# Two mixers that project the unnormed x: the norm's factor moves from the operands to the drains

## The chip, the cores and the metric

The kernel runs on one core of one Trainium2 chip. The metric is the device time of one execution of the program in microseconds (us), as the median of several runs. The engines are named as in the profile: PE (TensorE matmul) with PEld (its weight load), DVE (VectorE), ACT (ScalarE), POOL (GpSimd) and SP (SyncE), which here only issues DMAs.

## What is computed

A decoder trunk of two layers over 1024 tokens of width 1024, in float32. Cut to what matters:

```python
def rmsnorm(x, g):
    return x * rsqrt(mean(x * x, axis=-1) + EPS) * g

for l in range(2):
    if l == 1:
        shared = nsa_shared_kv(x, g_kv, w_kv, ...)         # norm of x, keys and values, compressed blocks
    mem_k, mem_v = split(rmsnorm(mem, g_mem[l]) @ w_mem_kv[l])   # 256 memory tokens, 4 heads of 128
    h = rmsnorm(x, g_mix[l])
    if l == 0:                                              # "mix A"
        q, k, v, r, alr, mq = split_cols(h @ a_w_in, [256, 256, 512, 512, 16, 512])
        log_a = log_sigmoid(alr @ w_alpha + b_alpha) / 16
        o = rmsnorm(gla_chunked(q, k, v, log_a), g_head) * silu(r)
    else:                                                   # "mix B"
        q, gates, mq = split_cols(h @ b_w_in, [512, 24, 512])
        o = nsa_attend(q, sigmoid(gates), *shared)
    x = x + concat([o, mem_attend(mq, mem_k, mem_v)]) @ w_out
    x = x + conv_ffn(rmsnorm(x, g_ffn[l]), ...)             # 1024 -> 2 x 2816 -> 1024
return rmsnorm(x, g_final)
```

The norm multiplies each token by one number, rs = 1 / sqrt(mean of squares + EPS). A projection is linear in its input, so (rs x g) @ W and rs (x g @ W) are the same but for rounding.

## The kernel before

**Tiles.** x stands with the 1024 channels as eight tiles of 128 partitions and the 1024 tokens as columns; all work goes in two halves of 512 tokens (`HT`), one after the other. A float32 product is made of three fast ones: each operand is split into a rounded part (`...r`, made on ACT) and the rest (`...l`, made on DVE: source minus rounded part), and PE multiplies r by r, r by l and l by r. So a weight tile of 128 x 1024 (`wtile`, `wload`) costs one ACT and one DVE pass (lines 176 and 177), a tile of h one ACT and one DVE pass of 512 columns (`rl`, lines 224, 225, or 227, 228 where a gain is multiplied in), and one projection of 128 output channels for one half (`projg`, lines 192 to 194) is 24 matmuls of 512 columns into one of eight PSUM banks. What takes the bank's result to SBUF is called its drain.

**The norm.** `Norm.add` squares a tile on ACT (line 256) and adds it up in two accumulators (`nacc`, line 266), one on DVE and the other on POOL where `pool` is true. `done` puts the sum over channels through PE (`ms`, line 278), and `inv_rms` (lines 239 to 244) makes rs as a tile of 128 equal rows, so a factor for each column. `gained` then makes hf = x rs for each of eight tiles, the odd ones on POOL, the others on DVE (line 285), and h is the split of hf.

**The stages, in order.** At the program's start `mix_a` projects the memory: `MemKV.project` multiplies the unnormed, split memory `mh` with four key weight tiles (`mk`: 96 matmuls of 256 columns) and then with four value weight tiles (`mv`: 48 of 512 columns), and takes the memory's norm in where it drains (`mkf`, line 363, and `mV`). Woven into it are the statistics (`stats`) and the normed h (`first_norm`) of x's first half. Then `qkv_a` projects keys and queries (`qk`, drained into `gk` and `gq`), the low rank gate input (`alr` into `aT`) and the values (`gv` into `vt`). For each half `gla` runs the gated linear attention: gate product z, cumulated sums b (lines 681 to 700), then seven levels, in each of which DVE makes an operand (`dec`, lines 709 to 715, and `z`, line 721), PE multiplies (`lev`, line 741) and DVE copies under a mask into `A` (line 748). Beside it `fill` yields other work of PE: the gates r (`gate_gen`: `gr` into `sr`), the memory queries (`mem_query`: `mq`), h and `qkv_a` of the second half. The output projection, the ConvFFN of layer 0 (`ffn`) and its `after_ffn0` follow. The last products of the ConvFFN are `dn` (`d` is the generator that yields them), drained by adding them to x (line 1348); beside them `after_ffn0` takes statistics, hf and h of both halves and the memory projection `MemKV(1)`. `mix_b` begins with `kc`, the keys and values that are to be compressed, and the branch gates, then memory queries, the selection's keys, values, queries `q2` and the attention. Output projection, ConvFFN of layer 1 and final norm close the program.

**What sets the order.** A scheduler puts each engine's instructions in a fixed row. It takes them from the generators in the order in which `weave` and `take` run them: `weave((a, 40.0), (b, 101.0))` draws from both so that they progress in step over their stated lengths. An engine works off its row strictly in order. Loads are issued by SP (weights, and x in `stats` by POOL), and the transfers of one issuer's queue follow each other. Buffers come from pools: 14 of 512 columns (`U`), 32 of 1024 (`V`), six for split weights (`wrl`), four for raw weights (`raw`).

Of the kernel before, what the change touches and what calls it, by code (L numbers as in the profile page):

```python
# [10 lines left out]
AF = mybir.ActivationFunctionType  # L11
# [23 lines left out]
def kernel(  # L35
# [88 lines left out]
    nc.gpsimd.dma_start(cs, cst)  # L124
# [111 lines left out]
    def inv_rms(ms, n):  # L236
        y = U(s="rs")
        a = U(s="rt")
# [8 lines left out]
    class Norm:  # L247
# [23 lines left out]
        def done(self):  # L271
            ms = PS("ms")[:, : self.w]
            if len(self.acc) == 2:
                nc.vector.tensor_tensor(self.acc[1], self.acc[1], self.acc[0], ALU.add)
                self.acc = self.acc[1:]
            n = len(self.acc)
            for j in range(n):
                mm(ms, on_d, self.acc[j], start=(j == 0), stop=(j == n - 1))
            return inv_rms(ms, self.w)

# [112 lines left out]
    class MemHead:  # L393
# [3 lines left out]
        def query(self, w, h):  # L397
            pq = PS("mq")
            yield from projg(pq, w, h)
            self.q = rl(pq, scale=-(P**-0.5), s="mq")  # L400
# [82 lines left out]
    def mem_query(mkv, jobs, att, gain=None):  # L483
        for hd, wsrc, hh in jobs:
            w = wtile(wsrc, "wmq", gain)
            for half, h in hh:
                m = MemHead(mkv, hd, half)
                yield from m.query(w, h)
# [100 lines left out]
    def mix_a():  # L589
        mkv = MemKV(0)  # L590
        mkv.load(nc.sync)
# [4 lines left out]
        def stats(half, xt):  # L596
            n = Norm(pool=half == 1)
            tvs = []
            for k2 in range(4):
                t = V(s="x0")  # L600
                tv = t.rearrange("p (k t) -> p k t", k=2)
                last_x[0] = nc.gpsimd.dma_start(tv, x[2 * k2 : 2 * k2 + 2, :, hs(half)].rearrange("k p t -> p k t"))
                tvs.append(tv)
            for tv in tvs:
                for i in range(2):
                    n.add(tv[:, i, :])
                    if half == 0:
                        xt.append(tv[:, i, :])
                    yield 1.0
            xt.append(n.done())  # L610
            yield 1.0

        def first_norm(half, h, xt):
            get = (lambda k: xt[k]) if half == 0 else reload(x, 1, nc.gpsimd)
            yield from gained(get, xt[-1], C_MIX, h)

        def qkv_a(h, after=None):
            kt, qt = V(s="gk"), V(s="gq")
            for q, t in enumerate((kt, qt)):
                for hp in range(2):  # L620
                    w = wtile(a_w[2 * (1 - q) + hp], "wqk")
                    ps = PS("qk")
                    yield from projg(ps, w, h)
                    src = ps.rearrange("p (c t) -> p c t", c=4)
                    dst = t.rearrange("p (c h t) -> p c h t", c=4, h=2)[:, :, hp, :]
                    nc.scalar.activation(dst, src, AF.Copy, scale=(1.0, 0.125)[q])
# [4 lines left out]
            nc.scalar.activation(aT[0:64, :], pa[0:64, :], AF.Copy)  # L631
# [23 lines left out]
        def gate_gen(h, sr):  # L655
            srv = [V(s="sr") for _ in range(2)]
            for r in range(4):
# [4 lines left out]
                nc.scalar.activation(s, ps, AF.Copy)  # L662
# [194 lines left out]
        xt = [[], []]  # L857

        def start():
            yield from stats(0, xt[0])  # L860
            yield from first_norm(0, h[0], xt[0])
# [5 lines left out]
        follow(nc.gpsimd.dma_start(idu, kst[:, : 2 * P]), last_raw[0], "order")  # L867
# [4 lines left out]
        weave((qkv_a(h[0], last_x[0]), 45.0), (stats(1, xt[1]), 12.0))  # L872
        om0 = []
        op0 = out_proj(a_wo, 0, x, nn[0], om0)
        for half in range(2):
            sr = []

            def fill():
                jobs = [(hd, a_w[8 + hd], [(half, h[half])]) for hd in range(4)]
                yield from gate_gen(h[half], sr)  # L880
                att = Attend(4)
                if half == 0:
                    both = blend(
                        (mem_query(mkv, jobs, att), 21.0), (later(15.0, first_norm(1, h[1], xt[1])), 15.0 + 10.0)
                    )
                    yield from beside(both, att, 4, 3)
                    yield from beside(qkv_a(h[1]), att, 0, 3)
                else:
                    yield from beside(mem_query(mkv, jobs, att), att, 4, 3)
# [4 lines left out]
            weave((gla(half, *self_out[half], sr), (40.0, 36.0)[half]), (fill(), (101.0, 84.0)[half]))  # L894
# [4 lines left out]
    def ffn(l, blocks_, after):  # L899
# [3 lines left out]
        nn = [Norm(w) for _, w in ends]  # L903
# [459 lines left out]
    def after_ffn0(d, nn, segs=None):  # L1363
        hh = [[], []]

        def prep(half):
            rs = nn[half].done()
            yield 1.0
            yield from gained(lambda k: xs[k][:, hs(half)], rs, None, hh[half], (1, 3, 5, 7))

        drain(take(d, 5))
        drain(take(d, 7))
        p0 = prep(0)
        mkv = MemKV(1)
        weave((take(d, 3), 8.1), (take(p0, 2), 2.0))
        mkv.load(nc.sync)
        mkv.square(nc.gpsimd)
        weave((d, 27.0), (take(p0, 5), 20.0))

        def both():  # L1380
            yield from p0
            yield 2.0
            yield from prep(1)

        weave((both(), 20.0), (mkv.project(), 36.0))
        for k in range(KT):
            xs[k] = None
        return mkv, hh

    def mix_b(mkv, h):  # L1390
# [15 lines left out]
        def comp_in(kind, half, ps):  # L1406
            pv = ps.rearrange("p (m j) -> p j m", j=16)
# [18 lines left out]
        for half in range(2):  # L1426
            for kind in range(2):
                ps = PS("kc")
                proj(ps, wkc[kind], h[half])
# [4 lines left out]
            nc.scalar.activation(t[0:64, :], pg[0:64, :], AF.Copy)  # L1434
            gsb.append(t)

# [20 lines left out]
        def keys(kind):  # L1457
            def evac(half, ps):
# [34 lines left out]
        def mem_all():  # L1493
            yield from beside(mem_query(mkv, mem_jobs, att, G_B), att, 5, 2)
# [3 lines left out]
        weave((mem_all(), 76.0), (compress(), 15.0))  # L1498
# [32 lines left out]
        def queries(m):  # L1531
            def evac(half, ps):
# [17 lines left out]
        def values(half, cs_):  # L1550
# [14 lines left out]
            for ps, c in zip(pv, cs_):  # L1565
                if val[half] is None:
                    val[half] = V(s="val")
                nc.scalar.activation(val[half][:, c * 256 : (c + 1) * 256], ps[:, :256], AF.Copy)
# [321 lines left out]
```

## Time and profile before

| | |
|---|---|
| median of 3 runs | 2359.45 us (2358.92 to 2360.3) |
| profiled execution | 2364.08 us |
| its span in the trace | 2362.0 us |
| PE busy | 2272.0 us, 96% |
| DVE busy | 1728.7 us, 73% |
| ACT busy | 1129.2 us, 48% |
| POOL busy | 506.7 us, 21% |

The profile comes from one execution, so times in it are compared with each other and with its own 2364.08 us. "Busy" is the time in which an engine has an instruction; a PE that is busy may still run at half its clock, which the granted clock shows (1.00 is the full one, and a mean below 1.00 in a stretch is a mix of the two levels, 2.4 and 1.2 GHz). A row of the timeline that ends in brackets names how long the engine had been idle before it and what released it. In names such as `mk<-mh,wmkr` the result stands left and the operands right.

### The profile page before, as it was taken

To read this page: it belongs to the slowest core of one execution; us is meant where nothing else is said; L and a number is where in the kernel's file an instruction comes from. 1 tells how busy PE (TensorE), PEld (TensorE's weight loads), DVE (VectorE), ACT (ScalarE), POOL (GpSimd) and SP (SyncE) were. 2 spreads that over 40 slices of the span, in tenths; PEclk is the share of its full clock that TensorE was granted. 3 is DMA by queue.
4 is the path that set the end of the run, shared out by engine and by line. 5 is a ranking of instruction groups with operands and counts; after the bars stand their busy time and mean duration, and the time that the engine had idled before them with its cause. 6 is when DMAs were issued, how large, how long until landed. Compare 5 with 4: busy or idle time off the path is not lost.

```text
span 2362.0 us, 31229 instructions
## 1 busy us (share of the span) xinstructions
PE 2272.0 (96%) x11030; PEld 1845.7 (78%) x11030; DVE 1728.7 (73%) x2988; ACT 1129.2 (48%) x2066; POOL 506.7 (21%) x429
## 2 busy tenths in 40 slices
PE   6989999999999999999899999999989999999997
PEld 5877877777788888887788877767777788888875
DVE  7496585978777768878555588874968777768786
ACT  6445544543343335455444588774543343335443
POOL 3222211313422210013202121110313422210011
PEclk9999999999999999999999999999999999999998
DMA  6213236433433229544231111017433433229432
GB/s 239 94 50 117 64 111 206 140 111 134 138 103 107 96 90 337 178 134 148 65 92 58 44 34 45 8 57 227 135 107 134 138 103 107 101 87 341 155 97 94
DMA packets 138221, 284.95 MB, mean 121 GB/s; under 512 B 16022, under 2 KB 22211, under 8 KB 138064
## 3 DMA queue, kind: packets, MB, share of 16 engines
q1 hardware_dynamic: 128992, 260.11, 33.5%
q0 software_dynamic: 4464, 14.46, 1.8%
q10 hardware_dynamic: 4608, 8.39, 1.0%
q8 instruction: 86, 1.41, 0.2%
q14 instruction: 71, 0.58, 0.1%
HBM read 211.06 MB, written 71.83 MB: 120 GB/s over the span
## 4 chain that ended last, share of the span: by engine, by line
PE 77%; DVE 11%; DMA 4%; issue 3%; ACT 3%; POOL 1%; SPq 1%; DVEq 0%; POOLq 0%; ACTq 0%
PE dn L1301 5%; PE dn L1302 5%; PE dn L1300 5%; PE fy L974 4%; PE fy L976 4%; PE fy L975 4%; PE no L1694 3%; PE fw L976 3%; PE fw L974 3%; PE fw L975 3%; PE fx L974 2%; PE fx L975 2%; PE fx L976 2%; PE npt L1678 2%; DMA wu<-in_w_up_dram 2%
## 5 line engine op out<-in xcount | busy, mean ns | idle before, releaser
L1300 PE MATMUL dn<-db,da 128*128 128x512 f32 (+1 forms) x628 | 243.0, 389 | 4.0 <-ACT db L1229 2.1
L1301 PE MATMUL dn<-db,da 128*128 128x512 f32 (+1 forms) x628 | 243.5, 388 | 2.6 <-DVE db L1230 2.6
L1302 PE MATMUL dn<-db,da 128*128 128x512 f32 (+1 forms) x628 | 243.3, 388 | 0.0
L974 PE MATMUL fy<-B,Ah 128*128 128x512 f32 x496 | 196.6, 396 | 14.9 <-DVE q L1008 7.5
L976 PE MATMUL fy<-B,Al 128*128 128x512 f32 x496 | 195.8, 395 | 2.5 <-DVE Al L939 2.5
L975 PE MATMUL fy<-B,Ah 128*128 128x512 f32 x496 | 195.1, 393 | 0.0
L938 ACT ACTIVATE Ah<-wu 128x1024 fp32r<-128x1024 f32 x124 | 130.3, 1052 | 108.5 <-PE fy L975 62.5
L958 POOL TENSOR_TENSOR wu<-wu,wu 128x512 f32<-128x512 f32 x44 | 61.3, 1394 | 558.6 <-DVE Al L939 305.0
L266 POOL TENSOR_TENSOR nacc<-nacc,nsq 128x512 f32<-128x512 f32 (+1 forms) x30 | 49.0, 1634 | 596.9 <-ACT nsq L256 596.7
L939 DVE TENSOR_TENSOR Al<-wu,Ah 128x1024 fp32r<-128x1024 f32 x124 | 160.7, 1297 | 20.7 <-ACT Ah L938 20.4
L1300 PEld LDWEIGHTS dn<-db,da 128*128 128x128 f32 x628 | 118.9, 189 | 29.1 <-issue 2.7
L1301 PEld LDWEIGHTS dn<-db,da 128*128 128x128 f32 x628 | 118.9, 189 | 27.6 <-DVE db L1230 3.3
L976 PE MATMUL fw<-B,Al 128*128 128x512 f32 x352 | 137.7, 391 | 0.0
L1302 PEld LDWEIGHTS dn<-db,da 128*128 128x128 f32 x628 | 118.7, 189 | 23.8 <-issue 0.2
L975 PE MATMUL fw<-B,Ah 128*128 128x512 f32 x352 | 137.1, 389 | 0.0
L974 PE MATMUL fw<-B,Ah 128*128 128x512 f32 x352 | 137.0, 389 | 0.0
L1230 DVE TENSOR_TENSOR db<-bl,db 128x512 fp32r<-128x512 f32 x154 | 107.9, 701 | 30.2 <-ACT db L1229 29.6
L974 PEld LDWEIGHTS fy<-B,Ah 128*128 128x128 f32 x496 | 94.1, 190 | 40.3 <-DVE q L1008 11.7
L976 PEld LDWEIGHTS fy<-B,Al 128*128 128x128 f32 x496 | 94.4, 190 | 24.5 <-DVE Al L939 4.4
L1229 ACT ACTIVATE db<-bl 128x512 fp32r<-128x512 f32 x154 | 95.7, 621 | 31.8 <-PE dn L1302 24.5
L975 PEld LDWEIGHTS fy<-B,Ah 128*128 128x128 f32 x496 | 94.1, 190 | 19.2
L192 PE MATMUL op<-om,wor 128*128 128x512 f32 x256 | 102.1, 400 | 0.9 <-ACT om L224 0.9
(416 smaller groups left out, 6289.5 us busy)
## 6 DMA issues: line engine op xcount, KB each, us to landing
wu<-in_w_up_dram SPq DMA_DIRECT2D x176, 256.0 KB, 2.9
bl<-gb_d SPq DMA_DIRECT2D x154, 256.0 KB, 2.8
gb_d<-fc SPq DMA_DIRECT2D x132, 256.0 KB, 3.0
wb<-in_w_down_dram SPq DMA_DIRECT2D x44, 256.0 KB, 4.2
wa<-in_w_down_dram SPq DMA_DIRECT2D x22, 512.0 KB, 7.8
xre<-om_d SPq DMA_DIRECT2D x32, 256.0 KB, 4.4
wo<-in_a_wo_dram SPq DMA_DIRECT2D x16, 512.0 KB, 3.6
x_r<-x SPq DMA_DIRECT2D x32, 256.0 KB, 2.5
```

The source lines that it names most:

```text
L192: mm(ps, wr[:, k, :], hr, start=(k == 0), stop=False)
L938: a = nc.scalar.activation(hi, src, AF.Copy)
L939: b = nc.vector.tensor_tensor(lo, src, f(hi), ALU.subtract)
L974: mm(ps, wr, hr, start=(first and j == 0), stop=False, skip_group_check=True)
L975: mm(ps, wr, hl, start=False, stop=False, skip_group_check=True)
L976: mm(ps, wl, hr, start=False, stop=(stop and j == 3), skip_group_check=True)
L1229: nc.scalar.activation(w[:, hs(0)], t, AF.Copy)
L1230: b = tt(w[:, hs(1)], t, f(w)[:, hs(0)], ALU.subtract)
L1300: mm(o, hi, bh, start=first, stop=False, skip_group_check=True)
L1301: mm(o, hi, bl, start=False, stop=False, skip_group_check=True)
L1302: mm(o, lo, bh, start=False, stop=stop or n == NP - 1, skip_group_check=True)
L1694: mm(acc[a * 64 : a * 64 + 64, :256], v, pf[:, a * 256 : (a + 1) * 256], start=(n == 0), stop=(n == last[a]),)
```

## The change

The norm's factor leaves the operands. h is now the split of x itself (in mix A of x times its gain column, which rides along in `rl`), and rs is multiplied in where PSUM is drained, as a product of the bank with the factor's tile on DVE. Values, whose drain has the tokens on the partitions, need the factor by token: `Norm.by_token` makes it with 16 small matmuls (`mst`, one column each) into `rst`, and ACT's drain takes it as its scale. With that hf and its products go, for 32 tiles of h.

The order moves too. At the start x's first half is loaded by SP, tile by tile, with the first weight tile `w0` behind the first; the first projection follows at once, and the statistics come behind h. The memory of layer 0 is loaded later, and its projection is the first thing that `fill` yields in the first GLA half. At the end of the ConvFFN of layer 0 h of the first half is taken while the `dn` products run; `kc` follows them directly, with h and the norm of the second half woven in; the memory projection of layer 1 comes later, in `mem_all`. In `ffn` and `stats` the norms' additions are all on DVE (`pool=False`), and the additions of the memory's norm of layer 1 move from POOL to DVE. The table of constants `cs` is loaded by ACT's queue instead of POOL's.

```diff
     def mix_a():
...
-        def stats(half, xt):
-            n = Norm(pool=half == 1)
+        def stats(half, h=None):
+            n = Norm(pool=False)
...
-                last_x[0] = nc.gpsimd.dma_start(tv, x[2 * k2 : 2 * k2 + 2, :, hs(half)].rearrange("k p t -> p k t"))
+                if half == 0:
+                    for i in range(2):
+                        last_x[0] = nc.sync.dma_start(tv[:, i, :], x[2 * k2 + i, :, hs(half)])
+                        if k2 + i == 0:
+                            w0.append(wraw(a_w[2], s="wqk"))
...
+                    if h is not None:
+                        h.append(rl(tv[:, i, :], col(C_MIX + 2 * k2 + i), s="h"))
...
+            rs[half] = n.done()
+            rst[half] = n.by_token()
...
+            def evac(ps, q, hp):
+                t = (kt, qt)[q]
+                src, sc = (a.rearrange("p (c t) -> p c t", c=4) for a in (ps, rs[half]))
+                dst = t.rearrange("p (c h t) -> p c h t", c=4, h=2)[:, :, hp, :]
+                nc.vector.scalar_tensor_tensor(dst, src, (1.0, 0.125)[q], sc, ALU.mult, ALU.mult)
...
-                    nc.scalar.activation(v[:, hs(i)], pv[2 * c2 + i], AF.Copy)
+                    c = 2 * c2 + i
+                    nc.scalar.activation(v[:, hs(i)], pv[c], AF.Copy, scale=rst[half][:, c : c + 1])
...
-                nc.scalar.activation(s, ps, AF.Copy)
+                nc.vector.tensor_tensor(s, ps, rs[half], ALU.mult)
...
-        pj, st = mkv.project(), start()
-        for g, n in ((pj, 1), (st, 4), (pj, 1), (st, 8 - 4), (pj, 1), (st, 1), (pj, 1)):
-            drain(take(g, n))
-        weave((pj, 16.0), (st, 16.0))
...
+        st = stats(0, h[0])
+        drain(take(st, 16))
...
+        qa = qkv_a(0, h[0], last_x[0])
+        drain(take(qa, 8))
+        drain(st)
+        mkv.load(nc.sync)
+        weave((qa, 38.0), (stats(1), 12.0))
...
-                yield from gate_gen(h[half], sr)
+                if half == 0:
+                    yield from mkv.project()
+                yield from gate_gen(half, h[half], sr)
...
-            weave((gla(half, *self_out[half], sr), (40.0, 36.0)[half]), (fill(), (101.0, 84.0)[half]))
+            weave((gla(half, *self_out[half], sr), (40.0, 36.0)[half]), (fill(), (132.0, 84.0)[half]))
...
-        nn = [Norm(w) for _, w in ends]
+        nn = [Norm(w, False) for _, w in ends]
...
     def after_ffn0(d, nn, segs=None):
...
+        drain(take(d, 9))
+        weave((take(d, 6), 16.2), (take_x(0, range(4)), 4.0))
+        weave((take(d, 4), 10.8), (take_x(0, range(4, 8)), 4.0))
+        drain(norm(0))
+        drain(d)
...
+        weave((front(0), 14.0), (second, 9.0))
+        mkv = MemKV(1)
+        mkv.load(nc.sync)
+        drain(front(1))
+        mkv.square(nc.vector)
...
-        weave((mem_all(), 76.0), (compress(), 15.0))
+        weave((mem_all(), 107.0), (compress(), 15.0))
```

The drains that are left out above read alike: `query` (16 tiles `mqs`), `comp_in` (4 `kcs`), the branch gates (2 `gsb`), `keys` (4 `ksf`) and `queries` (8 `qf`) each multiply the bank by `rs[half]` on DVE before what they did before, and `aT` (2) is such a product now.

Three places show the new order. First ACT at the program's start, before and then with the change; `wmkr` and `wqkr` are rounded parts of weight tiles, `mh` the split memory, `nacc` and `nsq` squares of x.

```order
L176 ACTIVATE wmkr_124<-wmk_93 128x1024
L227 ACTIVATE mh_103<-mem_95,cs 128x256 x2
L227 ACTIVATE mh_108<-mem_96,cs 128x256 x2
L227 ACTIVATE mh_113<-mem_97,cs 128x256 x2
L227 ACTIVATE mh_118<-mem_98,cs 128x256 x2
L327 ACTIVATE mem_95<-mem_95 128x512
```

```order
L256 ACTIVATE nacc_135<-x_1_93 128x512
L176 ACTIVATE wqkr_110<-wqk_95 128x1024
L256 ACTIVATE nacc_137<-x_1_93 128x512
L256 ACTIVATE nsq_139<-x_3_98 128x512
L227 ACTIVATE h_107<-x_1_93,cs 128x512
L227 ACTIVATE h_114<-x_1_93,cs 128x512
L227 ACTIVATE h_117<-x_3_98,cs 128x512
```

The memory's splits stood first; now three squares of x and one weight split stand ahead of the eight tiles of h, of which the first three are shown. Next DVE in the level stage of the first GLA half, before and then with the change; `dec` and `z` are a level's operands, `lev` its product, `wmql` and `wrl` weight splits, `mV` the memory's values, `sr` the gate's drain.

```order
L748 COPY_PREDICATED A_770<-umask,lev_934 128x8x64
L709 TENSOR_TENSOR dec_972<-b_854 128x64x8
L748 COPY_PREDICATED A_771<-umask,lev_935 128x8x64
L710 TENSOR_TENSOR dec_972<-b_854 128x64x8
L177 TENSOR_TENSOR wmql_1012<-wmq_1009,wmqr_1011 128x1024
L715 TENSOR_TENSOR dec_925<-dec_925,gk_443 128x32x16
L721 TENSOR_TENSOR z_929<-dec_925,gq_444 64x8x64
```

```order
L788 COPY_PREDICATED A_550<-umask,lev_833 128x8x64
L788 COPY_PREDICATED A_551<-umask,lev_834 128x8x64
L228 SCALAR_TENSOR_TENSOR mV_863<-mv_742,rs_676,mV_863 128x512
L228 SCALAR_TENSOR_TENSOR mV_866<-mv_743,rs_676,mV_866 128x512
L749 TENSOR_TENSOR dec_896<-b_725 128x64x8
L750 TENSOR_TENSOR dec_896<-b_725 128x64x8
L177 TENSOR_TENSOR wrl_975<-wr_972,wrr_974 128x1024
L788 COPY_PREDICATED A_550<-umask,lev_905 128x16x32
L755 TENSOR_TENSOR dec_896<-dec_896,gk_162 128x64x8
L761 TENSOR_TENSOR z_900<-dec_896,gq_163 64x8x64
L702 TENSOR_TENSOR sr_869<-gr_877,rs_223 128x512
```

Between the levels' operands stand now the memory's values, the gates' weight splits and the gates' drains, which were ACT's. Last DVE at the end of the first ConvFFN, before and then with the change; `x<-dn` is the drain of the last products, `wmkl` and `wmvl` the memory's weight splits, `wkcl` and `wg` those of the next stage, `kcs` a drain of `kc`.

```order
L1348 TENSOR_TENSOR x_6973<-dn_7763,x_6973 128x512
L266 TENSOR_TENSOR nacc_7978<-nacc_7978,nsq_8239 128x512
L285 TENSOR_TENSOR hf_8270<-x_6739,rs_8037 128x512
L266 TENSOR_TENSOR nacc_7978<-nacc_7978,nsq_8267 128x512
L274 TENSOR_TENSOR nacc_7978<-nacc_7978,nacc_7971 128x512
L177 TENSOR_TENSOR wmkl_8343<-wmk_8340,wmkr_8342 128x1024
L225 TENSOR_TENSOR h_8272<-hf_8270,h_8272 128x512
L225 TENSOR_TENSOR h_8306<-hf_8304,h_8306 128x512
L177 TENSOR_TENSOR wmkl_8396<-wmk_8393,wmkr_8395 128x1024
L177 TENSOR_TENSOR wmvl_8443<-wmv_8440,wmvr_8442 128x1024
```

```order
L244 TENSOR_TENSOR rs_8174<-rs_8174,rt_8175 128x512
L244 TENSOR_TENSOR rst_8187<-rst_8187,rtt_8188 128x4
L266 TENSOR_TENSOR nacc_7988<-nacc_7988,nsq_8206 128x512
L1389 TENSOR_TENSOR x_6985<-dn_7776,x_6985 128x512
L266 TENSOR_TENSOR nacc_7995<-nacc_7995,nsq_8220 128x512
L177 TENSOR_TENSOR wkcl_8272<-wkc_8268,wkcr_8271 128x1024
L266 TENSOR_TENSOR nacc_7988<-nacc_7988,nsq_8234 128x512
L1389 TENSOR_TENSOR x_6987<-dn_7777,x_6987 128x512
L213 TENSOR_TENSOR wg_8278<-praw_8275,wg_8278 128x8x24
L225 TENSOR_TENSOR h_8336<-x_6981,h_8336 128x512
L225 TENSOR_TENSOR h_8345<-x_6983,h_8345 128x512
```

Behind the last `dn` drain there stood hf, h and five splits of memory weights; now there stand the split of the next stage's second weight and the second half's last tiles of h.

## Rows read from the trace of the kernel before

**Rows 1.** Page: PE's busy us, share, instructions; PE's busy tenths by slice

```profile
PE 2272.0 (96%) x11030; PEld 1845.7 (78%) x11030; DVE 1728.7 (73%) x2988; ACT 1129.2 (48%) x2066; POOL 506.7 (21%) x429
...
PE   6989999999999999999899999999989999999997
```

**Rows 2.** Stretches: us, busy us by engine, granted PE clock, DMA share, GB/s

```profile
0.00:20.00 20.00, 10.24 (x59) 9.51 (x60) 11.98 (x28) 13.74 (x23) 6.14 (x14) 1.00 0.92 325
...
48.77:96.79 48.02, 48.02 (x211) 39.40 (x210) 20.63 (x22) 19.28 (x29) 11.75 (x13) 1.00 0.49 167
96.79:119.57 22.78, 20.64 (x109) 17.36 (x107) 10.99 (x12) 13.89 (x19) 6.53 (x6) 1.00 0.15 48
119.57:158.40 38.83, 34.93 (x188) 30.64 (x188) 36.55 (x45) 16.86 (x17) 12.23 (x11) 0.87 0.12 35
253.13:340.00 86.87, 83.30 (x456) 70.30 (x456) 67.95 (x97) 48.85 (x80) 21.03 (x13) 0.98 0.26 79
1074.40:1140.40 66.00, 52.75 (x256) 43.73 (x255) 60.65 (x74) 35.67 (x59) 30.40 (x20) 0.87 0.35 116
1169.60:1285.00 115.40, 115.10 (x660) 99.56 (x660) 60.81 (x110) 52.30 (x126) 16.73 (x28) 1.00 0.25 79
```

**Rows 3.** PE's timeline, program start: start, us, line, idle before, releaser

```profile
8.03 0.58 PE L192 MATMUL mk<-mh,wmkr 128*128 128x256 f32 x1 [8.03 <-ACT mh L227]
...
16.28 0.28 PE L192 MATMUL mk<-mh,wmkr 128*128 128x256 f32 x1
...
21.55 0.28 PE L194 MATMUL mk<-mh,wmkl 128*128 128x256 f32 x1
...
44.54 0.79 PE L377 MATMUL mv<-wmvl,mh 128*128 128x512 f32 x1 [2.80 <-DVE wmvl L177]
...
46.41 0.63 PE L376 MATMUL mv<-wmvr,mh 128*128 128x512 f32 x1
46.83 0.63 PE L377 MATMUL mv<-wmvl,mh 128*128 128x512 f32 x1
```

**Rows 4.** The same of ACT, DVE and POOL, program start

```profile
4.64 1.06 ACT L176 ACTIVATE wmkr<-wmk 128x1024 fp32r<-128x1024 f32 x1 [2.65 <-DMA wmk<-in_w_mk_dram]
...
16.08 1.06 ACT L176 ACTIVATE wmkr<-wmk 128x1024 fp32r<-128x1024 f32 x1 [0.30 <-DMA wmk<-in_w_mk_dram]
...
34.63 1.76 DVE L228 SCALAR_TENSOR_TENSOR h<-hf,cs,h 128x512 fp32r<-128x512 f32 x1
...
32.44 8.42 POOL L285 TENSOR_TENSOR hf<-x,rs 128x512 f32<-128x512 f32 x4 [24.17 <-DVE rs L244]
```

**Rows 5.** Groups of DVE and ACT, whole span: busy us, mean ns, idle

```profile
L177 DVE TENSOR_TENSOR wmkl<-wmk,wmkr 128x1024 fp32r<-128x1024 f32 x4 | 4.9, 1223 | 4.8 <-ACT wmkr L176 4.7
...
L363 DVE TENSOR_TENSOR mkf<-mk,rs 128x512 f32<-128x512 f32 x2 | 1.4, 678 | 0.0
...
L662 ACT ACTIVATE sr<-gr 128x512 f32<-128x512 f32 x8 | 4.7, 591 | 13.3 <-PE gr L194 13.3
```

**Rows 6.** Chain that ended last, first GLA half: start, us, what

```profile
96.79 0.86 PE z L681 x4
...
104.02 1.68 PE diag L690 x16
...
108.59 0.89 PE b L699 x8
```

**Rows 7.** PE's waits, first level stage: us in total, times, longest

```profile
PE lev L741 <- DVE z L721: 7.9, 3, 3.7
```

**Rows 8.** PE's waits, end of the first ConvFFN

```profile
PE mv L377 <- DVE wmvl L177: 7.5, 1, 7.5
PE dn L1301 <- DVE db L1230: 2.6, 1, 2.6
```

**Rows 9.** PE's timeline, last 25 us

```profile
2339.85 1.13 PE L278 MATMUL ms<-nacc,on_d 128*128 128x256 f32 x4 [0.67 <-POOL nacc L266]
...
2348.73 1.76 PE L278 MATMUL ms<-nacc,on_d 128*128 128x256 f32 x4 [3.49 <-POOL nacc L266]
```

More of the change, by code (lines that the diff above doesn't have):

```diff
@@ L279, in done, with by_token @@
             return inv_rms(ms, self.w)
+        def by_token(self):
+            n = self.w // P
+            pt = PS("mst")
+            for c in range(n):
+                for j, a in enumerate(self.acc):
+                    mm(
+                        pt[:, c : c + 1],
+                        a[:, c * P : (c + 1) * P],
+                        on_d[:, 0:1],
+                        start=(j == 0),
+                        stop=(j == len(self.acc) - 1),
+                    )
+            return inv_rms(pt[:, :n], n, S([P, 4], s="rst", bufs=3), S([P, 4], s="rtt", bufs=2))
     def gained(get, rs, gc, h, odd=(1, 3, 5, 7)):
@@ L487, in mem_query @@
                 m = MemHead(mkv, hd, half)
-                yield from m.query(w, h)
+                yield from m.query(w, h, rs[half])
                 att.heads.append(m)
@@ L609, in stats, with second_x @@
-                    yield 1.0
-            xt.append(n.done())
+                    yield 0.5
+            yield 2.0
+            rs[half] = n.done()
+            rst[half] = n.by_token()
             yield 1.0
[L613 to L617, printed above, removed]
-            kt, qt = V(s="gk"), V(s="gq")
-            for q, t in enumerate((kt, qt)):
+        def second_x(h):
+            get = reload(x, 1, nc.gpsimd)
+            for k in range(KT):
+                h.append(rl(get(k), col(C_MIX + k), s="h"))
+                yield 1.0
@@ L1363, in after_ffn0, with take_x, norm, second @@
     def after_ffn0(d, nn, segs=None):
[L1364 to L1390, printed above, removed]
+        rs, rst = [None] * 2, [None] * 2
+        def take_x(half, ks_):
+            for k in ks_:
+                hh[half][k] = rl(xs[k][:, hs(half)], s="h")
+                yield 1.0
+        def norm(half):
+            rs[half] = nn[half].done()
+            rst[half] = nn[half].by_token()
+            yield 0.5
+        hh = [[None] * KT, [None] * KT]
+        drain(take(d, 9))
[3 more added lines that the diff above has]
+        drain(d)
+        def second():
+            yield from take_x(1, (4, 5, 6, 7, 0, 1, 2, 3))
+            yield from norm(1)
+            for k in range(KT):
+                xs[k] = None
+        return second(), hh, rs, rst
+    def mix_b(second, h, rs, rst):
         G_KV, G_B = C_KV, C_MIX + 8
@@ L1425, in mix_b, with front @@
         gsb = []
-        for half in range(2):
+        def front(half):
             for kind in range(2):
                 ps = PS("kc")
-                proj(ps, wkc[kind], h[half])
+                yield from projg(ps, wkc[kind], h[half])
                 comp_in(kind, half, ps)
```

81 lines of the change are left out of this document (49 added, 32 removed).

## The prediction

> **What bounds the kernel now.** I read the page's busy shares and slices first: TensorE (PE) is busy 96% of the span, and the slices that fall below 9 are few [rows 1]. So time can only come out of the stretches where PE stands or runs at its half clock. The table of stretches shows where these are [rows 2]: the first 48.77 us, the level stage of the first GLA half (119.57 to 158.40, PE busy 34.93 of 38.83 us, granted clock 0.87) and the end of the first ConvFFN (1074.40 to 1140.40, 52.75 of 66.00 us, clock 0.87). In the stretch from 1169.60 to 1285.00 PE has no gap at all.
>
> I price a matmul by the stretch that never stops: 48.02 us for 211 records is 0.2276 us for 512 columns [rows 2]. At the half clock it is 0.43 us (46.41 to 46.83), and the 256-column matmuls of the memory keys take 0.12 us at full clock (16.28 to 21.55 holds 44 steps) [rows 3]. One memory projection is 96 such key matmuls and 48 value matmuls of 512 columns: 11.5 + 10.9, with the norm's few products about 23.3 us.
>
> **Where the start goes.** Until 48.77 us PE does only this 23.3 us of memory work and one matmul of the mixer. The first matmul comes at 8.03 us, and a value matmul waits 2.80 us until 44.54 [rows 3]. What it waits for is the chain of the norm: statistics, the product hf on VectorE (DVE) and GpSimd (POOL), the split h. The POOL products take 8.42 us for four, and DVE operations beside them stretch: one h takes 1.76 us beside POOL [rows 4], where a DVE product of this length takes 0.68 us alone [rows 5]. So some 25 us are lost ahead of 48.77.
>
> **The change, part by part.**
>
> *Program start.* The order on ScalarE (ACT) puts a square, the weight split, two squares and then the first h. These need x tiles 0 to 2 and one weight tile, 1.28 MB. The nearest row is the 512 KB load that now stands first in this queue: its ACT user starts at 4.64 [rows 4]. The remaining 0.77 MB at the 325 GB/s of the first 20 us [rows 2] take 2.4 us, so about 7.0, then one square and one h of about 0.6 us each, the 0.59 us of an ACT pass over 512 columns [rows 5]: PE starts near 8.2 us. Bounds: 6.5, if all lands with the first load, and 16, if it queues as a late load does (a split that waits for its load starts at 16.08 [rows 4]). From there PE has the 48.0 us that it now does between 48.77 and 96.79, one matmul, half clock for the first 7 us as now (3.4 us lost; 8.03 to about 15), about 1 us more for the second norm's products and 1 us of stalls: the gate product z of the first half, now at 96.79, comes at about 62. That is -34.8 us. The second weight tile's split stands behind eight h and five additions on DVE (13 x 0.68 = 8.8 us, so it is made near 18) and the first tile's matmuls are through near 17: that is the stall. The q and k drains wait on DVE behind eight mem splits, which wait for the mem loads, which stand on SP's queue behind three weight tiles; the value matmuls need these banks only near 38 us, some 3 us later than I find the drains done.
>
> *Memory keys inside the first GLA half.* The 23.3 us of work are not saved, only moved. From z to the first level product takes 22.78 us now [rows 2], and PE's work in it is 55 gate matmuls (12.5 us) and 5.2 us of the half's own products (z and b twice each, diag once [rows 6]). Afterwards the memory projection stands in place of the gate matmuls: 23.3 + 5.2, about 28.7 us and full: +5.9. In the level stage DVE is the limit: 36.55 us busy of 38.83 [rows 2], and the longest of PE's waits there end on DVE's z [rows 7]. The order puts four gate drains, two value splits and five more weight splits into it: 4 x 0.68 + 2 x 0.7 + 5 x 1.22 [rows 5], about 10 us, of which 2.3 fill idle time: +7.5. PE does 26 more matmuls in it, so 6.6 us of gate and query matmuls are left for the stretch behind, which is full: +6.6. Start and first half together: -34.8 + 5.9 + 7.5 + 6.6 = -14.8 us. Bounds: if no hole takes any of the moved work, -34.8 + 23.3 = -11.5, and less by what the level stage loses; if every hole takes some, -24.
>
> *The drains.* 52 PSUM drains that the norm's factor enters are DVE work now (8 q and k, 8 gate, 16 memory queries, 20 smaller or late ones); ACT had most of them at 0.59 us, and DVE's nearest row, a product of PSUM with a factor tile, is 0.68 us [rows 5]. Against them stand 16 hf on DVE and 16 on POOL that go. Outside the level stages DVE has room (60.81 of 115.40 us in the second mixer's queries [rows 2]), so I price them at nothing there; without that cover the 16 query drains would be 11 us. In the second GLA half (253.13 to 340, DVE 67.95 of 86.87, PE short by 3.6 us [rows 2]) four of them fall into the level stage: +1.5, bounds 0 and 5.
>
> Whether a drain beside a POOL product costs 0.68 or, as the h beside POOL, 1.76 us [rows 4, 5] decides up to 8 x 1.08 = 8.6 us of DVE time; I take 0.68, by the row of the same operand kinds. The Trainium skill ("SBUF — State Buffer", Who interferes with whom) says that a VectorE instruction with at most one SBUF input and no two-port mode doesn't contend with GpSimd. By that rule a drain with one PSUM operand keeps its 0.68 us and the 8.6 us stay out of the sum; h, with two SBUF inputs, is stretched in the trace as the rule has it.
>
> *End of the first ConvFFN.* From 1074.40 to 1140.40 PE has 102 down products, 96 key and 48 value matmuls: 23.2 + 11.5 + 10.9, with norms 46.8 us of 66.0, so 19.2 us are lost. PE waits 7.5 us for the last value weight split, which stands on DVE behind the norm's hf and h, and 2.6 us for an operand split [rows 8]. Afterwards the down products run into the compressed-key projection. Its first weight was split long before and h of the first half is made while the down products run; the second weight tile needs a buffer that the down products release, so its split, 1.06 us on ACT [rows 4] and 1.22 on DVE [rows 5], comes behind their end, against 5.5 us (24 x 0.2276) of matmuls that cover it. The second half's h (four late tiles, eight DVE operations of 0.68, near 6 us) and norm have 14.6 us of cover, half of the 29.2 us from 1140.40 to 1169.60 that now hold both halves of this projection and its gates. The memory projection follows some 30 us later with its weights loaded. I leave 2 us of loss and 0.9 us for new products: -16.3, bounds -18 and -11.
>
> *Additions out of POOL.* POOL's additions end PE's wait of 0.67 and 3.49 us before the last two statistics products [rows 9]. DVE is quicker at one but has them in line with the output products, and most of the 3.49 us is that line: I take the shorter wait off with a part lost, -0.5, bounds -1 and +0.5. The rest of the 18 additions that go to DVE lie beside a PE without a gap.
>
> **Sum.** -14.8 + 1.5 - 16.3 - 0.5 = -30.1 us. The profiled execution took 2364.08 us (span 2362.0), 4.6 above the median of the runs; I take the difference off the median: 2359.45 - 30.1 = 2329.3.
>
> **The rivals.**
>
> *A, DVE gives the start back.* For it: the level stage is DVE's already. Price: no hole takes the memory work (-11.5), the four drains stretch there (+4.3), and the second half costs 5: -7.2 + 5 - 16.3 - 0.5 = -19.0, so 2340.4. Against it: between z and the first level product DVE is busy only 10.99 of 22.78 us [rows 2].
>
> *B, the junction doesn't close.* The second weight split or the late h come late and the clock falls to half as it does now: -6 in place of -16.3, so 2339.6. Against it: the cover of 5.5 and 14.6 us above.
>
> *C, the start isn't as early.* The x tiles now stand in one queue with the weights; if PE starts at 16 us, 8 us are given back: about 2337. The Trainium skill ("DMA: Bandwidth & Descriptors", Issuing engines are not separate DMA queues) says that loads of all issuing engines share the same 16 DMA engines and that spreading them saves only issue time. By it the move of x to SP's queue gains no rate, only another order; the sum takes nothing for it either.
>
> *D, slower.* Each drain now stands in DVE's queue, and a projection whose bank isn't drained holds PE. If all 52 are waited for by their own length, 52 x 0.68 = 35.4 us go on top: 2364.7. It decides only where all eight banks are taken. For it: DVE is 94% busy in the level stage. Against it: no wait of PE for a bank is among its waits [rows 7, 8].
>
> **How the numbers follow.** Chances: the forecast 0.68, A 0.14, B 0.07, C 0.07, D 0.04. The forecast's own bounds, with the head's 9 us either way and the junction's, give about 2319 to 2340; reaching over A, B and C the range is 2319 to 2346. The measurement of this kernel can tell about 0.2% (4.7 us) from no change. All but D are faster by more than that; I leave 0.03 for a pile-up of A, B and C that ends within it: faster 0.92, same 0.03, slower 0.05.
>
> **What would show it.** In the profile of the changed kernel: PE's first mixer matmul near 8 us, z near 62; DVE over 90% busy in the first level stage, which takes 45 us or so; PE without a gap over 2 us behind the last down product; DVE's drains at 0.68 us. Wrong would be: PE waits that end on a drain of qk, gr, mq or kc, a first matmul behind 12 us, or a level stage over 50 us.

## The result, and the profile after

The changed kernel takes 2343.52 us (median of four runs, 2342.43 to 2347.28) where the kernel before takes 2359.88 us beside it: a ratio of 0.9931, interval 0.9914 to 0.9948. The forecast was 2329.3 us, 30.1 us less; 16.4 us less came. Beside the first experiments the changed kernel ran again: 2337.46 us against 2362.10, a ratio of 0.9903 (0.9879 to 0.9928), 24.6 us less. So the gain is 16 to 25 us. The direction is the one that was forecast; the size falls short by 5.5 to 13.7 us.

The page of the changed kernel, PE's busy line and its slices, answers to [rows 1]: the first slice, 6 tenths before, has 8 now.

```profile
PE 2264.1 (97%) x11062; PEld 1842.3 (79%) x11062; DVE 1743.6 (74%) x3065; ACT 1130.0 (48%) x2054; POOL 442.2 (19%) x383
...
PE   8999999999999999999899999999999999999997
```

Where the time went is read by laying the starts of the same PE products in two traces of each kernel side by side. The table takes differences of such starts; "moved" is the memory projection's 23.3 us, which lies in other stretches afterwards.

| stretch on PE | before (two traces) | changed (two traces) | change | predicted |
|---|---|---|---|---|
| start to first gate product z | 96.6, 100.6 | 64.6, 65.5 | -32.0 to -35.1 | -34.8 |
| z to first level product | 22.9, 22.9 | 28.6, 28.6 | +5.6 | +5.9 |
| level stage, from there to kdT | 39.1, 37.7 | 41.3, 41.3 | +2.2 to +3.5 | +7.5 |
| kdT to z of the second half | 94.3, 94.0 | 98.4, 98.3 | +4.0 to +4.4 | +6.6 |
| from there to the first ConvFFN | 194.7, 197.6 | 198.8, 197.0 | -0.7 to +4.1 | +1.5 |
| its first dn to gateT, moved work put back | 282.5, 282.2 | 267.9, 268.1 | -14.1 to -14.6 | -16.3 |
| gateT to the first query product, moved work taken off | 113.5, 113.5 | 128.2, 127.0 | +13.5 to +14.7 | 0 |
| both ConvFFNs, first product to first dn | 878.6, 878.6 | 877.0, 873.2 | -1.6 to -5.4 | 0 |
| second ConvFFN's first dn to the last ms | 224.2, 222.4 | 219.7, 221.3 | -1.2 to -4.5 | -0.5 |

One row stands out, and alone it is as large as the shortfall of the first measurement: what the end of the first ConvFFN gave was given back in the stage behind it. Of the other rows, the start and the first half gave 5 to 7 us more than forecast (z of the second half comes 20.1 and 21.6 us earlier, for 14.8), and the two ConvFFNs, in which the change touches nothing up to the first dn, gave 1.6 us in one trace of the changed kernel and 5.4 in the other; nine more traces with the change, or most of it, have 872.3 to 874.5 us there. The ConvFFNs' gain is unforeseen. PE's products are the same 1850 in each. PE is idle for 22.0 and 23.8 us of the two in the traces before and for 22.4 and 20.1 afterwards, and its granted clock is at the half level for 17.1 and 13.7 us before, for 13.7 and 10.2 afterwards. PE's busy time less half of that is 847.8 to 848.1 us in all four. So the gain is made of less time at the half clock and, in the second trace, of shorter waits; what shortens these is open.

The stretches of the changed kernel, with the columns of [rows 2]: z to the first level product, the level stage, kc to gateT, and two that begin at gateT.

```profile
64.62:93.21 28.59, 28.59 (x192) 26.41 (x190) 19.69 (x24) 17.70 (x25) 4.24 (x2) 1.00 0.37 111
93.21:134.49 41.28, 38.79 (x228) 33.81 (x227) 41.28 (x52) 20.58 (x20) 17.30 (x15) 1.00 0.34 105
...
1084.16:1115.08 30.92, 30.92 (x140) 25.13 (x138) 15.29 (x31) 23.27 (x42) 1.15 (x2) 1.00 0.37 134
1115.08:1130.48 15.40, 7.23 (x41) 6.94 (x41) 9.82 (x14) 9.78 (x16) 0.00 (x0) 0.70 0.14 45
...
1115.08:1266.61 151.53, 140.99 (x804) 122.48 (x803) 94.23 (x151) 72.23 (x150) 18.72 (x26) 0.96 0.29 91
```

PE has no gap from kc to gateT, as foreseen; the 19 us of [rows 2] are closed. But in the 15.40 us behind gateT it is busy for 7.23 us, at a granted clock of 0.70. PE's timeline shows the waits, at the start, in the level stage and at gateT:

```profile
9.71 0.79 PE L192 MATMUL qk<-h,wqkr 128*128 128x512 f32 x1 [9.71 <-ACT h L227]
...
19.58 0.51 PE L194 MATMUL qk<-h,wqkl 128*128 128x512 f32 x1 [0.89 <-DVE wqkl L177]
...
98.11 0.50 PE L194 MATMUL gr<-h,wrl 128*128 128x512 f32 x1 [2.49 <-DVE wrl L177]
...
1125.93 1.90 PE L1497 MATMUL gateT<-fold,gsb 64*128 64x24 f32 x8 [8.17 <-DVE gsb L1479]
```

The last is the one that counts: the second half of the gate transposes waits 8.17 us for gsb, a drain of 0.68 us whose bank had been full since 1115. What held it is seen in the timelines of ACT, and then of DVE, in this stretch:

```profile
1092.27 0.91 ACT L227 ACTIVATE mh<-mem,cs 128x256 fp32r<-128x256 f32 x2 [3.67 <-DMA mem<-in_mem_dram]
1093.09 0.64 ACT L1458 ACTIVATE ck<-kcs 64x256 f32<-64x256 f32 x1
...
1098.26 2.51 ACT L227 ACTIVATE mh<-mem,cs 128x256 fp32r<-128x256 f32 x6
...
1106.38 1.16 ACT L341 ACTIVATE mem<-mem 128x512 f32<-128x512 f32 x2
...
1121.48 0.63 ACT L1458 ACTIVATE ck<-kcs 64x256 f32<-64x256 f32 x1 [1.95 <-DVE kcs L1450]
...
1108.82 0.69 DVE L241 SCALAR_TENSOR_TENSOR rt<-ms,rs 128x512 f32<-128x512 f32 x1 [6.35 <-ACT rs L240]
...
1120.77 0.68 DVE L1450 TENSOR_TENSOR kcs<-kc,rs 128x512 f32<-128x512 f32 x1
1124.06 1.23 DVE L1465 TENSOR_TENSOR ck<-ck,pe 128x1024 f32<-128x1024 f32 x1 [2.60 <-ACT ck L1459]
1125.20 0.68 DVE L1479 TENSOR_TENSOR gsb<-gate,rs 64x512 f32<-64x512 f32 x1
```

gsb stands on DVE behind an addition to ck, and that waits for ACT's copies into ck. ACT has 32 copies to make here, and ahead of them and between them now stand the memory's eight splits (the first waits 3.67 us for its load), its four squares and three weight splits: the memory projection brought them along when it was moved behind kc. The same row delays the factor that the drains now need: PE begins the second half's statistics (ms) at 1098.68, but ACT comes to its part of rs only at 1107.44, behind eight more copies and three squares, and DVE stands 6.35 us for it until 1108.82. kcs and gsb of this half can't come before rs is there.

### The profile page after: what moved, and what is told of

It is laid out like the page before. It is cut to its first block, busy times and chain, and to the rows that moved or that the text cites. A ratio compares the mean times of both kernels' runs of the same rounds, so it can differ in the third digit from the quotient of the medians.

```text
span 2341.0 us, 31315 instructions
## 1 busy us (share of the span) xinstructions
PE 2264.1 (97%) x11062; PEld 1842.3 (79%) x11062; DVE 1743.6 (74%) x3065; ACT 1130.0 (48%) x2054; POOL 442.2 (19%) x383
## 4 chain that ended last, share of the span: by engine, by line
PE 75%; DVE 13%; DMA 4%; ACT 3%; issue 3%; POOL 1%; SPq 1%; DVEq 0%; POOLq 0%; ACTq 0%
PE dn L1342 5%; PE dn L1341 5%; PE dn L1343 5%; PE fy L1017 5%; PE fy L1015 4%; PE fy L1016 4%; PE no L1753 3%; PE fw L1017 3%; PE fw L1016 3%; PE fw L1015 3%; PE npt L1737 2%; PE fx L1015 2%; PE fx L1016 2%; PE fx L1017 2%; PE sc L1680 2%
## 5 line engine op out<-in xcount | busy, mean ns | idle before, releaser
L1015 PE MATMUL fy<-B,Ah 128*128 128x512 f32 x496 | 197.0, 397 | 16.7 <-DVE q L1049 8.7
L1017 PEld LDWEIGHTS fy<-B,Al 128*128 128x128 f32 x496 | 94.2, 190 | 23.8 <-DVE Al L980 4.0
L1016 PEld LDWEIGHTS fy<-B,Ah 128*128 128x128 f32 x496 | 94.3, 190 | 19.2
L1270 ACT ACTIVATE da<-wb 128x512 fp32r<-128x512 f32 x88 | 55.1, 629 | 98.4 <-PE dn L1342 61.3
```

The source lines that it names most:

```text
L1015: mm(ps, wr, hr, start=(first and j == 0), stop=False, skip_group_check=True)
L1016: mm(ps, wr, hl, start=False, stop=False, skip_group_check=True)
L1017: mm(ps, wl, hr, start=False, stop=(stop and j == 3), skip_group_check=True)
L1270: nc.scalar.activation(w[:, hs(0)], t, AF.Copy)
```

## The experiments

**The changed kernel again.** 

> The changed kernel once more, beside the runs that vary it. Theory: its time is 2342 to 2346 us, the last gate transposes (gateT) again wait some 8 us for gsb, and from gateT to the first query product (q) 151 us pass. Rival (the loss behind gateT is one execution's accident): that wait is under 3 us in this trace.

2337.46 us, less than the 2342 to 2346 expected; the wait of gateT is 8.01 us, from gateT to q 150.30 us pass. The loss belongs to the kernel.

**The gate ahead of kc.** In the second half only:

```diff
+            if half == 1:
+                gate()
             for kind in range(2):
                 ps = PS("kc")
                 yield from projg(ps, wkc[kind], h[half])
                 comp_in(kind, half, ps)
+            if half == 0:
+                gate()
```

> In the second half of the front of the second mixer the gate's products and their drain gsb stand ahead of the two kc products. Theory (ACT's row holds gsb back: gsb stands on DVE behind the additions to ck, and these wait for ACT's 32 copies and the memory's splits): the 8.2 us wait of gateT goes, at most half of it comes back where the next user of ck or of a weight split waits, so 4 to 8 us less than the changed kernel: 2336 to 2340. Rival (the stage behind gateT is slow by the memory work that was moved into it, whatever the gate does): within 1.5 us of the changed kernel.

2331.30 us, 6.2 less than the changed kernel beside it. The wait of gateT is gone; 3.46 us of it come back, at the memory's norm:

```profile
1131.29 0.67 PE L353 MATMUL mms<-macc,on_d 128*128 128x256 f32 x2 [3.46 <-DVE macc L347]
```

**kcs in its readers' order.**

```diff
-            nc.vector.tensor_tensor(t, ps, rs[half], ALU.mult)
-            pv = t.rearrange("p (m j) -> p j m", j=16)
+            pv = t.rearrange("p (j m) -> p j m", j=16)
+            src, sc = (a.rearrange("p (m j) -> p m j", j=16) for a in (ps, rs[half]))
+            nc.vector.tensor_tensor(t.rearrange("p (j m) -> p m j", j=16), src, sc, ALU.mult)
```

> kcs is written in the order in which the copies to ck read it, so the copies read runs of 32 neighbouring values in place of every 16th. Theory (a copy costs 0.64 us because it reads SBUF in steps of 64 bytes; from PSUM it cost 0.38): the 32 copies fall to 0.40 or less, ACT gets some 8 us free, the wait of gateT falls from 8.2 to under 3 us, 4 to 8 us less in all; kcs itself may rise from 0.69 to 1.2 us. Rival (reading SBUF costs this much in any order): copies stay at 0.63, time within 1.5 us of the changed kernel.

2332.87 us, 4.6 less; the wait of gateT falls to 3.06 us, about as expected. The groups of ACT's copies (busy us, mean ns) in the kernel before, with val beside them, in the changed kernel and here, and DVE's kcs in the last two (in each kernel one of the two lines that make 16 copies each):

```profile
L1414 ACT ACTIVATE ck<-kc 64x256 f32<-64x256 f32 x16 | 6.1, 380 | 11.8 <-PE kc L194 11.6
...
L1568 ACT ACTIVATE val<-nv 128x256 f32<-128x256 f32 x8 | 2.8, 383 | 0.7 <-PE nv L1563 0.7
```

```profile
L1458 ACT ACTIVATE ck<-kcs 64x256 f32<-64x256 f32 x16 | 10.2, 637 | 5.0 <-DVE kcs L1450 4.9
...
L1450 DVE TENSOR_TENSOR kcs<-kc,rs 128x512 f32<-128x512 f32 x4 | 2.7, 685 | 0.0
```

```profile
L1459 ACT ACTIVATE ck<-kcs 64x256 f32<-64x256 f32 x16 | 6.6, 415 | 5.6 <-DVE kcs L1452 5.5
...
L1452 DVE TENSOR_TENSOR kcs<-kc,rs 128x512 f32<-128x512 f32 x4 | 4.4, 1093 | 0.0
```

So the change itself made the copies dear. Before, they read every 16th value out of PSUM, 380 ns each; now they read every 16th value out of an SBUF tile, 637 ns, and over 32 copies that is 8.2 us of ACT. Reading runs of 32 neighbours takes 415 ns. The four kcs pay 0.41 us each for writing in steps. The Trainium skill ("SBUF — State Buffer", Door 1) says that SBUF has lines of 16 bytes and that each access which goes to a new line pays a penalty; a step of 64 bytes does so each time. The trace agrees for ACT reading SBUF (637 against 415 ns); out of PSUM the step cost nothing, since val, 256 columns read in order there, takes 383 ns.

**Both.** 

> Both: gate ahead and kcs in the order of its readers. Theory: no wait of gateT over 1 us, and the hidden units (hid) don't wait either; 151 us from gateT to q become 140 to 144, time 2331 to 2337. If the two only remove the same wait, j3 is no faster than the better of j1 and j2; then what is left of the loss lies elsewhere in this stage (rival).

2326.85 us (2326.59 to 2327.00), 10.6 less than the changed kernel and under the 2331 to 2337 expected, ratio to the kernel before 0.9856 (0.9838 to 0.9875). From kc on PE has no wait over 0.8 us until 1249 us, and the stretch from gateT to q takes:

```profile
1112.80:1252.20 139.40, 137.20 (x804) 119.33 (x803) 91.06 (x148) 66.94 (x144) 18.92 (x26) 1.00 0.29 92
```

That is 12.1 us less than the 151.53 of the changed kernel: 8.3 us of gaps (10.5 against 2.2) and 3.8 us of PE's busy time for the same 804 records, which ran at a clock of 1.00 where it had been 0.96. The gap cost its own length and the half clock behind it. The two edits are not one and the same: 6.2 and 4.6 alone, 10.6 together. With the moved work taken off, 116.1 us are left for 113.5 in the kernel before, so 2.6 us of the loss remain.

**The kernel before, a second trace.** 

> The kernel before, once more, for a second trace. If the last stage's gain (224.2 us from the first dn of the second ConvFFN to the last ms before, 219.6 to 222.2 in the traces since) belongs to the change, this trace shows 223 to 225 us there; if it is the one execution's, 220 to 222. From gateT to q it shows 113.5 us again.

The last stage takes 222.4 us and gateT to q 113.5. That is between the two expectations for the last stage, so the first trace's 224.2 was in part its own.

**Additions back on POOL.**

```diff
-        nn = [Norm(w, False) for _, w in ends]
+        nn = [Norm(w) for _, w in ends]
```

> The changed kernel with the norms' additions at the ConvFFNs' ends on POOL again, as before. Theory A (the tail's gain comes from these additions): 2 to 4 us slower than the changed kernel, and the last ms waits for POOL 3 us or more. Theory B (as predicted, DVE has them in line with the output products and little is won): within 1 us of the changed kernel.

2343.62 us, 6.1 above the changed kernel's 2337.46, on another chip and with 4.6 us of the difference between the traces ahead of the first ConvFFN, where this edit does nothing; in the first measurement the changed kernel took 2343.52 us too. So the whole times can't tell, and the last stage has to. It takes 223.7 us; the ten traces with the additions on DVE have 219.6 to 222.2 (mean 220.5), the three with POOL, the two of the kernel before among them, 222.4 to 224.2 (mean 223.4). PE's timeline from the first dn on, with the additions on POOL, has the waits of [rows 9] again, and two ahead of them that the kernel before has as well; below it, the changed kernel's:

```profile
2273.38 1.12 PE L278 MATMUL ms<-nacc,on_d 128*128 128x512 f32 x2 [1.61 <-DVE nacc L274]
...
2291.61 0.47 PE L1341 MATMUL dn<-db,da 128*128 128x512 f32 x1 [1.88 <-DVE x L1306]
...
2320.95 1.13 PE L278 MATMUL ms<-nacc,on_d 128*128 128x256 f32 x4 [0.68 <-POOL nacc L266]
...
2329.83 1.34 PE L278 MATMUL ms<-nacc,on_d 128*128 128x256 f32 x4 [3.49 <-POOL nacc L266]
```

```profile
2292.55 0.47 PE L1341 MATMUL dn<-db,da 128*128 128x512 f32 x1 [2.12 <-DVE x L1306]
...
2327.45 1.13 PE L278 MATMUL ms<-nacc,on_d 128*128 128x256 f32 x4 [2.50 <-DVE nacc L266]
2329.42 1.20 PE L278 MATMUL ms<-nsq,on_d 128*128 128x256 f32 x2 [0.84 <-ACT nsq L256]
```

These waits add up to 7.7 and 5.5 us. PE's idle time in this stage is 7.6 to 7.7 us in all three traces with POOL and 5.5 to 5.7 in the ten with DVE, so the additions on DVE are worth about 2 us here: the wait at the first half's statistics (1.61) is gone, and those at the last ones are 0.8 us shorter. The rest of the scatter lies in PE's busy time, in traces with the same waits.

**The memory projection as a block ahead of the first GLA half.**

```diff
         weave((qa, 38.0), (stats(1), 12.0))
+        drain(mkv.project())
...
-                if half == 0:
-                    yield from mkv.project()
                 yield from gate_gen(half, h[half], sr)
```

with the weave's length back at 101. 

> The changed kernel with the memory projection of layer 0 as a block of its own between qkv_a and the first GLA half, where the gates are the filler again. Theory (woven into the half it takes the place of gate products and fills PE's gaps in the level stage): z comes 23.3 us later, z to the first level product takes 23 in place of 28.6 us, the level stage 39 to 42 us, and 8 to 12 us are lost in all. Rival (the place doesn't matter, the start's gain is all in not waiting for the norm): within 2 us of the changed kernel.

Its ten runs scatter from 2346.19 to 2362.63 (median 2354.50); the fastest is 10.6 us above the changed kernel's fastest, the median 17.0 above its median, and why they scatter is open. In the trace of one of its fastest runs the z of the second half comes 9.9 to 10.7 us later (243.55 against 233.65 and 232.85). Stretches from z to the first level product and of the level stage:

```profile
109.64:150.19 40.55, 33.26 (x186) 28.39 (x184) 40.55 (x51) 16.72 (x17) 16.92 (x15) 0.92 0.25 78
87.87:109.64 21.77, 21.77 (x114) 18.61 (x113) 12.88 (x16) 13.39 (x18) 1.57 (x1) 1.00 0.24 75
```

The start alone brings z from 96.6 (100.6 in the second trace) to 87.9, so 9 to 13 us; the weave is worth 10 more. The level stage is nearly as long with 186 PE records as with the 228 of the changed kernel. DVE is busy throughout in both, and the changed order puts 42 more products beside it.

**Two drains back on ACT.** The norm's factor is left out of the gates and memory queries of the first mixer here:

```diff
-                nc.vector.tensor_tensor(s, ps, rs[half], ALU.mult)
+                nc.scalar.activation(s, ps, AF.Copy)
...
+            if self.mkv.l == 0:
+                self.q = rl(pq, scale=-(P**-0.5), s="mq")
```

> The changed kernel with the gates' and the memory queries' drains of the first mixer on ACT as before; the norm's factor is left out of these two. Theory (DVE is the limit of both level stages, and the drains stand in its row between the levels' operands): the first level stage, 41.3 us, becomes 38 to 40, z to kdT of the second half, 73.6 us in the first trace of the changed kernel, goes back to 69 to 71, in all 4 to 7 us less than the changed kernel. Rival (the drains fill idle time on DVE, and the second half lost its 3 us to something else): within 1.5 us.

2337.75 us, for 2337.46 of the changed kernel on another chip (0.9902 and 0.9903 of the kernel before): no change. The first level stage and the second half's stretch up to kdT here, and then in the second trace of the changed kernel:

```profile
93.66:134.95 41.29, 38.78 (x228) 33.78 (x226) 40.79 (x49) 22.39 (x24) 19.17 (x12) 1.00 0.31 96
...
233.29:303.77 70.48, 66.90 (x369) 57.53 (x368) 56.11 (x76) 38.77 (x58) 20.25 (x12) 0.98 0.19 60
```

```profile
94.03:135.31 41.28, 38.77 (x228) 33.79 (x227) 41.28 (x52) 20.68 (x20) 18.01 (x15) 1.00 0.35 111
...
233.65:305.48 71.83, 66.05 (x369) 56.23 (x368) 60.30 (x83) 36.93 (x54) 21.76 (x12) 1.00 0.19 56
```

The level stage doesn't move at all, the second half gives 1.35 us. So the theory of this run falls: the drains are not what the level stages cost more. In the first, PE is busy for 38.78 of the 41.29 us and short by one wait of 2.5 us for a weight split (98.11 above), with the drains on either engine.

**The best version again, and an earlier h.** In the second of these the squares of x's first half are ordered behind the second h on ACT:

```diff
+            if self.behind is not None:
+                follow(i, self.behind, "order")
```

> The kernel with gate ahead and kcs in its readers' order once more, beside the next: 1.3 to 1.6% faster than the kernel before, z near 64 us.

> The same with the squares of x's first half held behind the second h on ACT. Theory (PE's late first matmul, 9.7 for 8.2 us as predicted, is the third square's wait for its x tile, which stands ahead of h): first matmul at 7.5 to 8.2 us, z 1 to 2 us earlier, time 1 to 2 us less. Rival (later statistics and weight splits give it back): z within 0.5 us of the other.

2328.83 and 2329.24 us: the same. The first matmul comes at 7.41 us instead of 10.73, but z at 66.10 instead of 65.65:

```profile
7.41 0.80 PE L192 MATMUL qk<-h,wqkr 128*128 128x512 f32 x1 [7.41 <-ACT h L229]
...
18.73 0.68 PE L192 MATMUL qk<-h,wqkr 128*128 128x512 f32 x1 [2.95 <-ACT wqkr L176]
```

The second weight split now stands behind all eight squares, and PE waits for it. The rival holds: here the first matmul isn't what sets z.

**x issued by POOL.**

```diff
-                        last_x[0] = nc.sync.dma_start(tv[:, i, :], x[2 * k2 + i, :, hs(half)])
+                        last_x[0] = nc.gpsimd.dma_start(tv[:, i, :], x[2 * k2 + i, :, hs(half)])
```

> The changed kernel with x's first half issued by POOL instead of SP, the order of the loads otherwise kept; ACT's row then has two squares ahead of the first h. Theory (another issuer gains no rate, only another order): first matmul between 7.5 and 10.5 us, z within 1.5 us of the changed kernel's 64.6 to 65.5. Rival (SP's queue is what makes the start early): first matmul behind 12 us.

One run, 2342.36 us. First matmul at 10.40, z at 67.31, 1.9 to 2.7 us behind the changed kernel: more than the 1.5 us that I gave it, far less than the rival. Over the first 20 us 268 GB/s are moved with either issuer. ACT's first square waits for its x tile until 7.53 us, where SP as issuer has it at 4.50:

```profile
7.53 0.63 ACT L256 ACTIVATE nacc<-x 128x512 f32<-128x512 f32 x1 [5.08 <-DMA x<-in_x_dram]
```

## Why the prediction fell short

- **Start: right, 3 us late; start and first half together better than forecast** (-20.1 and -21.6 us up to z of the second half, for -14.8). z came at 64.6 and 65.5 for 62, with PE's first matmul at 9.7 and 10.6 for 8.2; the stretch behind it took 28.59 us for 28.7, full as worked out. (The half clock that I put at the start is not in the granted clock, which reads 1.00 there [rows 2]; it is read from the spacing of the matmuls, in the changed kernel 0.43 us up to 14.92 and 0.23 behind it.)
- **Level stage and the stretch behind it: priced too high.** I added DVE's moved work to the level stage (+7.5; its parts add up to 7.9) as if it were PE's; it cost 2.2 to 3.5. DVE is indeed full (41.28 of 41.28 us), but the memory work and the gates kept PE supplied: it did 38 products more, worth 8.6 us, stood 2.5 us instead of 4.1, and its clock stayed at 1.00 where [rows 2] had 0.87. Four of the later traces have some half clock and 42.6 to 42.8 us there. I had two readings wrong. The gate products between z and the first level product are 67, not 55, and PE did 38 more in the level stage, not 26; the two errors cancel, so 29 were left for the stretch behind, as forecast. But that stretch was not full: PE had stood 1.7 us in it, and it cost 4.0 to 4.4 for 6.6. And the three waits of 7.9 us in [rows 7] are those of both halves; the first half has two of 5.8 us, one of them ahead of its first level product. The drains, which I put among the stage's load, cost it nothing (the run with two drains on ACT).
- **The drains: priced right where I looked.** The rows of the changed kernel have 0.67 to 0.69 us for them, and the second half's +1.5 is close to that run's 1.35, one trace against one (the two traces of the kernel before differ by 2.1 us in that stretch). POOL's work beside them did not stretch them. The drains priced at nothing that were not free are kcs, by what it did to its reader, and gsb, by what stood ahead of it.
- **End of the first ConvFFN: right up to gateT, 2 us too much** (-14.1 to -14.6 for -16.3), by the step as it stood: PE runs into kc without a gap.
- **Behind gateT: this is the step that failed.** I wrote that the memory projection follows with its weights loaded, and counted what moved with it for PE alone. Its eight splits, four squares and weight splits moved too, into ACT's row between the copies that hid and gsb wait for, and the change made those copies 0.26 us longer each. 14 us went back. The sign that I named for this place, no gap of PE over 2 us behind the last down product, failed with one of 8.17. My rival B put such a loss at the second weight split or the late h; neither is late. The place was one stage further on, and the runs with the gate ahead and with kcs in order show it: 10.6 of the 14 us come back. The share of the dearer copies was tried alone (4.6 us); that the memory's work in ACT's row makes the rest is read from the timelines, and no run takes that work alone out of it. With both edits the kernel stands 30 to 35 us below the one before. That this is the sum I forecast is in part luck: the start and first half, the ConvFFNs and the tail gave more than their terms, the end of the first ConvFFN gave less.
- **Tail: right in sign, too small**: about 2 us for 0.5. I had looked at the last two waits alone and not at the one ahead of them, which went.
- **The rivals.** **A** (DVE gives the start back) did not come. **C** neither: the start was early by whatever issuer, within 2.7 us. **D** (drains waited for) came at one drain, gsb, and there by what stood ahead of it and not by its own length.
- **The range held by luck.** 2343.5 us lies outside the bounds that I gave the forecast itself (2319 to 2340); the range reached so far only over A, B and C, none of which came. The second measurement, 2337.5, lies inside both, as gains that I had not foreseen made up for a part of the loss.

## What to carry to other kernels

When a block of work is moved, count what it issues on every engine at the new place, and look there for the row that others wait on: here PE's books balanced and ACT's did not. A factor multiplied in at a drain is cheap as an instruction, but the intermediate tile can change what the next reader pays; let the writer of such a tile take the step, once, and its many readers read neighbours. A PE gap costs its length and then the half clock behind it: with 8.3 us of gaps went 3.8 us of slowed products.

## What the runs showed of the hardware that I had not expected

A 64 x 256 copy on ACT that reads every 16th value takes 380 ns out of PSUM and 637 ns out of SBUF; 415 ns out of SBUF in runs of 32 neighbours. DVE's product of 128 x 512 takes 0.69 us when it writes in order and 1.09 us when it writes every 32nd place. And a level stage that DVE fills wholly (41.28 of 41.28 us) took 42 more PE products than the one of the run with the memory projection as a block (40.55 us), at 0.7 us more, with the granted clock at 1.00 for 0.92.
